# Attention scores as 64-row products of two heads, one run per key chunk, behind a hold

## The chip, the cores and the metric

The kernel runs on one core of one Trainium2 chip. The metric is the device time of one execution in microseconds (us); the time before is the median of three runs, 2896.34 us (2895.69 to 2900.71).

A core has TensorE (PE; its weight loads are listed as PEld), VectorE (DVE), ScalarE (ACT), GpSimd (POOL) and a queue engine (SP) that issues the transfers. PE writes its results to PSUM, eight banks of 512 float32 columns on 128 partitions, and each engine takes its instructions in a fixed order.

## What is computed

Two layers over 2048 tokens with 16 learned meta tokens in front, model width 1024, all in float32. Layer 0 runs sliding-window attention and a convolution branch side by side. Layer 1, which the change is about, is stick-breaking attention with 16 heads of 64:

```python
z = jnp.einsum('bqhd,bkhd->bhqk', qp[:, i * BLOCK:kend], kp[:, :kend]).astype(jnp.float32) * scale
log_beta = jax.nn.log_sigmoid(z)
log_1m = jnp.where(valid, jax.nn.log_sigmoid(-z), 0.0)
after = lax.cumsum(log_1m, axis=3, reverse=True) - log_1m
a = jnp.where(valid, jnp.exp(log_beta + after), 0.0)
outs.append(jnp.einsum('bhqk,bkhd->bqhd', a.astype(v.dtype), vp[:, :kend]))
```

Each query's weight on a key is sigmoid(z) of that key times the product of sigmoid(-z) over all later keys. The output is gated by SiLU, projected, normalized and added to the input.

## The kernel before

Matrix products whose precision matters are split: an operand is a high part in the short float32r format plus a low part, and `mm3` adds high x high, low x high and high x low. A projection unit is one output block of 128 features for up to 512 tokens: 8 x 3 = 24 products into one PSUM tile `pj`, then read by ACT (`ev`), and for most kinds by DVE.

Layer 1 works by head pair `p` (0 to 7; two heads `h`, 64 rows each) and half of the tokens `hf`. Inside, `pair_steps(m)` takes 256 queries (two blocks `x` of 128) and walks their keys backwards in chunks of at most four blocks of 128 (`edges`), which gives 8 chunks for a head pair in the first half of the tokens and 16 in the second, 192 in all. One chunk has four score tiles, `(h, x)`. For each:

- PE: `z` (L912), two products of 128 rows. The stationary side is a query tile that holds the high (then the low) part of one head's queries twice, in rows 0 to 63 and 64 to 127; the moving side `kst` holds that head's keys, high part above low part. So one product gives high x high plus high x low.
- ACT: two sigmoids of it, `om` (L919) and `be` (L920). POOL masks the diagonal block in a pair's first chunk (L923).
- DVE: a scan along the keys, `S` (L925), then `be` times `S` (L926).
- PE: transposes of `be` into `pt` (L944); ACT copies them to `aT` (L950).

When all four are through, PE multiplies the transposed weights with the values into `av` (L958). Those products use half of the array's columns each, one head in either half (`128*64` in the profile). A row's `128*128` or `128*64` gives the rows and columns of the array that a product takes.

The order on each engine is made by a scheduler at build time, from the order of the calls, from priorities (`high_priority`) and from its own estimate of times. `interleave` calls projection units of a later head pair between the chunks of the current one; `behind` ties a unit to the value products of a few chunks before. A PSUM tile waits for the last reader of the tile that had its bank. The banks before are `pj` 2, `pz` 3 (scores), `pt` 2 (transposes), `pav` 1.

Of the kernel before, what the change touches and what calls it, by code (L numbers as in the profile page):

```python
# [18 lines left out]
P = 128  # L19
# [16 lines left out]
PB = (2, 3, 2)  # L36
# [42 lines left out]
class Trunk:  # L79
# [113 lines left out]
    def layer0(self, after=None):  # L193
# [300 lines left out]
        def cbranch(ut):  # L494
# [44 lines left out]
            def pw():  # L539
# [91 lines left out]
        def outp(t):  # L631
# [3 lines left out]
            def mm(nh):  # L635
# [9 lines left out]
                ps = self.bank("pj", "po")  # L645
# [92 lines left out]
    def after0(self, pool, tags):  # L738
        self.layer1_pools()
        self.evs = (pool, tags, D, 2)  # L740
        self.H, self.gates, self.tags = {}, [], cycle(("raw", "wh", "wl", "wh", "wl"))
# [9 lines left out]
        def proj(p, hf, parts=(0, 1)):  # L751
# [11 lines left out]
            def unit(m, part, c0, n, evac):  # L763
                def go():
# [4 lines left out]
                    ps = self.bank("pj", "pj1")  # L769
# [54 lines left out]
    def layer1(self):  # L824
# [12 lines left out]
        def attn(p, hf):  # L837
# [43 lines left out]
            def qload(m):  # L881
                q0 = NM + m * 2 * P
                S["q"] = qs = []
                for h in range(2):
                    for i in range(2):
                        qt = w2.tile([P, 256], F32R, tag=f"q{h}{i}", name="qt")
                        for j in range(2):
                            self.mv(qt[j * HD : j * HD + HD], qd[i][p, h * HD : h * HD + HD, q0 : q0 + 256])
                        qs.append(qt)

            def pair_steps(m):
# [5 lines left out]
                def chunk(ei):  # L897
# [6 lines left out]
                    nbs = [b1 - b0 - (1 if first else 0), b1 - b0]  # L904
                    for h in range(2):
                        for x in range(2):
# [3 lines left out]
                            z = self.bank("pz", "z")  # L910
                            for i in range(2):
                                nc.tensor.matmul(z[:, :n], S["q"][2 * h + i][:, x * P : x * P + P], S["k"][h][:, k0 : k0 + n], start=(i == 0), stop=(i == 1))  # L912
# [7 lines left out]
                            nc.scalar.activation(be[:, :n], z[:, :n], AF.Sigmoid, scale=0.125)  # L920
# [10 lines left out]
                    cps, avs = [], []  # L931
                    for c in range(0, b1 - b0, 2):
                        cw = min(2, b1 - b0 - c)
                        aTs = []
                        for h in range(2):
# [9 lines left out]
                            aT = w4.tile([P, 512], F32, tag="aT", name="aT")  # L945
# [5 lines left out]
                            aTs.append(aT)  # L951
# [182 lines left out]
```

## Time and profile before

| | |
|---|---|
| Median of three runs | 2896.34 us (2895.69 to 2900.71) |
| Profiled execution, its own time | 2902.22 us |
| Its span, first to last instruction | 2900.5 us |
| Granted TensorE clock in it, mean | 0.982 |
| Busy: PE, PEld, DVE, ACT, POOL | 2735.1, 2193.5, 2209.4, 1472.3, 777.6 us |
| Score products (L912) | 1536, 394.9 us busy |
| Transposes (L944) | 2176, 363.2 us busy |
| Value products (L958) | 2304, 282.0 us busy |
| Scans (L925) | 536.6 and 204.8 us busy in two groups |

A group's row reads: line, engine, operation, tile written and tiles read, shapes, count, busy time, mean of one in ns, then the idle time before them on that engine with what ended it. A timeline row reads: start, duration, engine, line, operation, tiles, count; neighbours of one kind are merged. PE's durations overlap, because a product starts before the one ahead of it has left the array, so its busy time overstates how full it is: what a product costs is the distance between starts.

### The profile page before, as it was taken

The page shows a single profiled execution, that of the slowest core. Times are in us where ns is not written, and L with a number is a line of the kernel's source. Part 1 is how long each engine was busy: PE and PEld are TensorE (multiplying, and loading weights), DVE is VectorE, ACT ScalarE, POOL GpSimd, SP SyncE. Part 2 cuts the span into 40 slices and gives each one's busy share as a digit, 9 for nine tenths or more (in the row PEclk, how much of TensorE's full clock was granted, in tenths as well). Part 3 has the DMA queues.
Part 4 walks back from the last instruction along what each step waited for, and adds up shares of the span by engine and source line. Part 5 has one row for each costly group of instructions (what it writes and reads, how often), then busy time and mean ns, then how long its engine had stood idle before and what let it go on. Part 6 is the DMA issues. An engine that isn't in the chain of part 4 may idle for free.

```text
span 2900.5 us, 49605 instructions
## 1 busy us (share of the span) xinstructions
PE 2735.1 (94%) x16110; PEld 2193.5 (76%) x16110; DVE 2209.4 (76%) x3696; ACT 1472.3 (51%) x3574; POOL 777.6 (27%) x2679
## 2 busy tenths in 40 slices
PE   7888999999899999999999899999999999999997
PEld 7886777777688799888887677777777777766876
DVE  7987888888767744666668987878888887887864
ACT  4223434343545323455445656666666766665551
POOL 3431212000000212333335532323223322333210
PEclk9999999999999999999999999999999999999999
DMA  7877888788876664444446462423232342244322
GB/s 258 283 251 221 254 267 256 234 241 267 235 209 187 213 199 146 130 127 137 128 137 182 130 178 65 113 76 101 66 103 88 88 111 73 74 129 126 113 95 91
DMA packets 303986, 462.87 MB, mean 160 GB/s; under 512 B 46640, under 2 KB 200640, under 8 KB 300656
## 3 DMA queue, kind: packets, MB, share of 16 engines
q1 hardware_dynamic: 303728, 459.70, 52.5%
q8 instruction: 129, 2.11, 0.3%
q14 instruction: 129, 1.06, 0.1%
HBM read 312.16 MB, written 142.14 MB: 157 GB/s over the span
## 4 chain that ended last, share of the span: by engine, by line
PE 71%; DVE 10%; DMA 7%; issue 4%; ACT 4%; POOL 2%; SPq 1%; DVEq 0%; ACTq 0%; POOLq 0%
PE pj L142 11%; PE pj L144 11%; PE pj L143 11%; PE z L912 8%; PE av L958 7%; PE pt L944 7%; PE po L142 4%; PE po L144 4%; PE po L143 4%; DVE y L309 3%; DVE S L925 2%; DMA qs<-qr 1%; DVE be L926 1%; DMA raw<-in_w_in 1%; ACT om L919 1%
## 5 line engine op out<-in xcount | busy, mean ns | idle before, releaser
L925 DVE TENSOR_TENSOR_SCAN S<-om,be 128x401 f32<-128x401 f32 (+3 forms) x512 | 536.6, 1069 | 71.9 <-ACT om L919 51.3
L919 ACT ACTIVATE om<-z 128x384 f32<-128x384 f32 (+5 forms) x768 | 377.9, 510 | 196.7 <-PE z L912 131.8
L926 DVE TENSOR_TENSOR be<-be,S 128x385 f32<-128x385 f32 (+5 forms) x768 | 413.6, 563 | 76.0 <-POOL be L917 22.2
L142 PE MATMUL pj<-th,wh 128*128 128x512 f32 (+2 forms) x1280 | 460.5, 360 | 7.1 <-DVE ev L810 3.6
L144 PE MATMUL pj<-th,wl 128*128 128x512 f32 (+2 forms) x1280 | 452.8, 354 | 0.0
L143 PE MATMUL pj<-tl,wh 128*128 128x512 f32 (+2 forms) x1280 | 450.5, 352 | 0.0
L950 ACT COPY aT<-pt 128x512 f32<-128x512 f32 (+2 forms) x672 | 334.2, 504 | 196.6 <-PE pt L944 156.2
L912 PE MATMUL z<-kst,qt 128*128 128x384 f32 (+6 forms) x1536 | 394.9, 357 | 31.2 <-ACT be L920 29.8
L920 ACT ACTIVATE be<-z 128x384 f32<-128x384 f32 (+5 forms) x768 | 375.5, 505 | 72.7 <-PE pt L944 72.0
L309 DVE SCALAR_TENSOR_TENSOR y<-u,cw,y 128x512 f32<-128x512 f32 (+1 forms) x480 | 391.7, 828 | 6.1
L944 PE MATMUL pt<-ident,be 128*128 128x128 f32 x2176 | 363.2, 282 | 17.4 <-ACT ev L799 7.7
L944 PEld LDWEIGHTS pt<-ident,be 128*128 128x128 f32 x2176 | 253.6, 142 | 113.0 <-issue 31.0
L912 PEld LDWEIGHTS z<-kst,qt 128*128 128x128 f32 x1536 | 247.7, 190 | 75.7 <-ACT be L920 55.3
L958 PE MATMUL av<-aT,vt 128*64 128x256 f32 (+1 forms) x2304 | 282.0, 380 | 4.3 <-DVE og L976 4.3
L916 POOL MEMSET om<- 128x1 f32 x768 | 74.8, 99 | 768.6 <-DVE S L925 753.5
L144 PE MATMUL pj<-hTh,wl 128*128 128x512 f32 (+2 forms) x704 | 246.7, 353 | 23.9 <-POOL wl L132 16.9
L142 PEld LDWEIGHTS pj<-th,wh 128*128 128x128 f32 x1280 | 241.8, 189 | 33.9 <-DVE ev L810 4.6
L144 PEld LDWEIGHTS pj<-th,wl 128*128 128x128 f32 x1280 | 241.0, 188 | 29.9
L143 PEld LDWEIGHTS pj<-tl,wh 128*128 128x128 f32 x1280 | 241.4, 189 | 25.1 <-issue 0.4
L142 PE MATMUL pj<-hTh,wh 128*128 128x512 f32 (+2 forms) x704 | 249.6, 356 | 8.9 <-DMA wh<-wk 4.6
L925 DVE TENSOR_TENSOR_SCAN S<-om 128x257 f32<-128x257 f32 (+4 forms) x256 | 204.8, 812 | 63.1 <-POOL om L923 50.3
L143 PE MATMUL pj<-hTl,wh 128*128 128x512 f32 (+2 forms) x704 | 246.8, 351 | 0.8 <-DVE hTl L191 0.8
(184 smaller groups left out, 4702.2 us busy)
## 6 DMA issues: line engine op xcount, KB each, us to landing
raw<-in_w_in SPq DMA_DIRECT2D x98, 512.0 KB, 4.0
wr<-wk SPq DMA_DIRECT2D x44, 512.0 KB, 6.2
wh<-wk SPq DMA_DIRECT2D x44, 512.0 KB, 5.2
wl<-wk SPq DMA_DIRECT2D x44, 512.0 KB, 6.5
qt<-qhd SPq DMA_DIRECT2D x256, 64.0 KB, 2.6
qt<-qld SPq DMA_DIRECT2D x256, 64.0 KB, 2.4
wk<-wh SPq DMA_DIRECT2D x22, 512.0 KB, 4.9
wk<-wl SPq DMA_DIRECT2D x22, 512.0 KB, 4.9
```

What stands on the lines that cost most here:

```text
L142: mm(out, sh, mh, start=first, stop=False)
L143: mm(out, sh, ml, start=False, stop=False)
L144: mm(out, sl, mh, start=False, stop=last)
L309: return lambda: nc.vector.scalar_tensor_tensor(y[:, :TC], u[:, w : w + TC], cw[:, j, w : w + 1], y[:, :TC], ALU.mult, ALU.add)
L912: nc.tensor.matmul(z[:, :n], S["q"][2 * h + i][:, x * P : x * P + P], S["k"][h][:, k0 : k0 + n], start=(i == 0), stop=(i == 1))
L919: nc.scalar.activation(om[:, :n], z[:, :n], AF.Sigmoid, scale=-0.125)
L920: nc.scalar.activation(be[:, :n], z[:, :n], AF.Sigmoid, scale=0.125)
L925: nc.vector.tensor_tensor_scan(P_[:, : n + 1][:, ::-1], om[:, : n + 1][:, ::-1], om[:, : n + 1][:, ::-1], init, ALU.mult, ALU.bypass)
L926: nc.vector.tensor_tensor(bl[:, : n + 1], bl[:, : n + 1], P_[:, : n + 1], ALU.mult)
L944: nc.tensor.transpose(pt[:, o : o + P], bes[h, x][:, mo + b * P : mo + b * P + P], self.ident)
L950: cps.append(nc.scalar.copy(aT[:, lo:hi], pt[:, lo:hi]))
L958: mi = nc.tensor.matmul(av[h * HD : h * HD + HD, qc0 + x0 : qc0 + 256], S["v"][:, b0 + b, h * HD : h * HD + HD], at, start=not S["started" ...
```

## The change

The score products are cut to 64 rows. The query tiles are now one for the high and one for the low part with both heads, head 0 in rows 0 to 63 and head 1 below, and so are the key tiles. For each block `x`, three products per head (high x high, high x low, low x high) are called in turn for the two heads, each head in its half of the array's rows and with a PSUM bank of its own. All products of a chunk are called ahead of its sigmoids, in one run of twelve. The first of them gets a wait for the last four readings of score banks (`zread`) and for the copies of the transposes of the chunk ahead's first head (`half`). The transposes are called head by head. PSUM is split anew: `pj` 1, `pz` 4. Projections in layer 0, and the output projections outside of attention, alternate between `pj` and `pz`; those among attention use the one `pj` bank.

```diff
-PB = (2, 3, 2)
+PB = (1, 4, 2)
...
-                    ps = self.bank("pj", "pw")
+                    ps = self.bank(next(banks), "pw")
...
-                ps = self.bank("pj", "po")
+                ps = self.bank(next(banks), "po")
...
+        self.zread, self.half, self.free = [], [], cycle(BK)
...
-                    ps = self.bank("pj", "pj1")
+                    ps = self.bank(next(self.free), "pj1")
...
-                for h in range(2):
+                for i in range(2):
                     kst = w4.tile([P, T], F32R, tag="kst", name="kst")
-                    for i in range(2):
-                        self.mv(kst[i * HD : i * HD + HD, :n], kd[i][p, h * HD : h * HD + HD, :n])
+                    self.mv(kst[:, :n], kd[i][p, :, :n])
...
-                for h in range(2):
-                    for i in range(2):
-                        qt = w2.tile([P, 256], F32R, tag=f"q{h}{i}", name="qt")
-                        for j in range(2):
-                            self.mv(qt[j * HD : j * HD + HD], qd[i][p, h * HD : h * HD + HD, q0 : q0 + 256])
-                        qs.append(qt)
+                for i in range(2):
+                    qt = w2.tile([P, 256], F32R, tag=f"q{i}", name="qt")
+                    self.mv(qt, qd[i][p, :, q0 : q0 + 256])
+                    qs.append(qt)
...
+                    zs, wait = {}, self.zread[-4:] + self.half
+                    for x in range(2):
+                        n = nbs[x] * P + mo
+                        if n == 0:
+                            continue
+                        for h in range(2):
+                            zs[h, x] = self.bank("pz", "z")
+                        for i, j in ((0, 0), (0, 1), (1, 0)):
+                            for h in range(2):
+                                r = slice(h * HD, h * HD + HD)
+                                mi = nc.tensor.matmul(zs[h, x][:, :n], S["q"][i][r, x * P : x * P + P], S["k"][j][r, k0 : k0 + n], start=(i + j == 0), stop=(i == 1))
+                                if wait is not None:
+                                    self.after_all(mi, wait)
+                                    wait = None
...
-                            z = self.bank("pz", "z")
-                            for i in range(2):
-                                nc.tensor.matmul(z[:, :n], S["q"][2 * h + i][:, x * P : x * P + P], S["k"][h][:, k0 : k0 + n], start=(i == 0), stop=(i == 1))
+                            z = zs[h, x]
...
-                            nc.scalar.activation(be[:, :n], z[:, :n], AF.Sigmoid, scale=0.125)
+                            self.zread.append(nc.scalar.activation(be[:, :n], z[:, :n], AF.Sigmoid, scale=0.125))
...
-                    for c in range(0, b1 - b0, 2):
-                        cw = min(2, b1 - b0 - c)
-                        aTs = []
-                        for h in range(2):
+                    cps, aTs = [], {}
+                    for h in range(2):
+                        for c in range(0, b1 - b0, 2):
+                            cw = min(2, b1 - b0 - c)
...
+                        if h == 0:
+                            self.half = cps[:]
...
-                ps = self.bank("pj", "po1")
+                ps = self.bank(next(self.free), "po1")
...
+        self.free = cycle(("pj",))
         for p in range(2, 6):
             interleave(proj(p, 0), attn(p - 2, 0))
...
+        self.free = cycle(BK)
         for t in range(8, NT):
```

How this moves the work shows in the order on PE. In the rows, `z` are score products (with the lengths of their key rows), `pt` transposes, `av` value products, `pj` projections; a count at the end merges equal neighbours. First a place in the second half of the tokens where no projection unit is called. Before:

```order
L912 MATMUL z<-kst,qt 128x400 x2
L944 MATMUL pt_24352<-ident,be 128x128 x4
L912 MATMUL z<-kst,qt 128x256 x2
L912 MATMUL z<-kst,qt 128x384 x2
L958 MATMUL av_24083<-aT,vt_23339 64x256 x8
L944 MATMUL pt_24359<-ident,be 128x128 x4
L912 MATMUL z<-kst,qt 128x256 x2
L944 MATMUL pt_24366<-ident,be 128x128 x4
```

Now:

```order
L913 MATMUL z<-kst,qt 128x400 x12
L953 MATMUL pt_20045<-ident,be 128x128 x3
L953 MATMUL pt_20052<-ident,be 128x128 x3
L953 MATMUL pt_20160<-ident,be 128x128 x4
L969 MATMUL av_19877<-aT,vt_19865 64x256 x8
L953 MATMUL pt_20167<-ident,be 128x128 x2
L953 MATMUL pt_20172<-ident,be 128x128 x4
L953 MATMUL pt_20179<-ident,be 128x128 x2
L913 MATMUL z<-kst,qt 128x256 x6
```

Before, the next chunk's scores (256 and 384 columns) stand between the transposes of the chunk ahead, tile by tile. Now the chunk's own transposes (`pt_20160` and after) all stand ahead of the next chunk's scores.

Second, a place where a projection unit ends. Before:

```order
L944 MATMUL pt_24729<-ident,be 128x128 x2
L142 MATMUL pj_24938<-th_18069,wh_24820 128x512
L143 MATMUL pj_24938<-tl_18070,wh_24820 128x512
L144 MATMUL pj_24938<-th_18069,wl_24821 128x512
L142 MATMUL pj_24938<-th_18069,wh_24820 128x512
L143 MATMUL pj_24938<-tl_18070,wh_24820 128x512
L144 MATMUL pj_24938<-th_18069,wl_24821 128x512
L912 MATMUL z<-kst,qt 128x512 x2
L944 MATMUL pt_24788<-ident,be 128x128 x4
L912 MATMUL z<-kst,qt 128x400 x4
L958 MATMUL av_24083<-aT,vt_23339 64x256 x6
```

Now:

```order
L953 MATMUL pt_20293<-ident,be 128x128 x3
L953 MATMUL pt_20300<-ident,be 128x128
L143 MATMUL pj_20491<-tl_17399,wh_20487 128x512
L144 MATMUL pj_20491<-th_17398,wl_20488 128x512
L953 MATMUL pt_20304<-ident,be 128x128 x4
L953 MATMUL pt_20311<-ident,be 128x128
L913 MATMUL z<-kst,qt 128x384 x12
L969 MATMUL av_19877<-aT,vt_19865 64x256 x4
```

Before, the last scores of one chunk and then scores of the next follow the unit, around transposes of the chunk ahead. Now the unit, the transposes of both heads, the twelve scores of the next chunk and the value products stand in line.

More of the change, by code (lines that the diff above doesn't have):

```diff
@@ L944, in chunk @@
                                         nc.tensor.transpose(pt[:, o : o + P], bes[h, x][:, mo + b * P : mo + b * P + P], self.ident)
-                            aT = w4.tile([P, 512], F32, tag="aT", name="aT")
+                            aTs[h, c] = aT = w4.tile([P, 512], F32, tag="aT", name="aT")
                             if nbs[0] < c + cw and cw == 2:
@@ L950, in chunk @@
                                 cps.append(nc.scalar.copy(aT[:, lo:hi], pt[:, lo:hi]))
-                            aTs.append(aT)
-                        for b in range(c, c + cw):
-                            o = (b - c) * 256
-                            x0 = 0 if b < nbs[0] else P
-                            avs += [(h, b, x0, aTs[h][:, o + x0 : o + 256]) for h in range(2)]
+                        if h == 0:
+                            self.half = cps[:]
+                    avs = []
+                    for b in range(b1 - b0):
+                        c, x0 = b - b % 2, 0 if b < nbs[0] else P
+                        o = (b - c) * 256
+                        avs += [(h, b, x0, aTs[h, c][:, o + x0 : o + 256]) for h in range(2)]
                     with tc.high_priority(offset=AVP):
```

1 line of the change is left out of this document (removed).

## The prediction

> **What bounds the kernel now.** I read the page's busy shares and chain first, then busy time by stage, the groups of the attention stage, and the timeline of one pass.
>
> ```profile
> PE 2735.1 (94%) x16110; PEld 2193.5 (76%) x16110; DVE 2209.4 (76%) x3696; ACT 1472.3 (51%) x3574; POOL 777.6 (27%) x2679
> PE 71%; DVE 10%; DMA 7%; issue 4%; ACT 4%; POOL 2%; SPq 1%; DVEq 0%; ACTq 0%; POOLq 0%
> 1269.00:1346.00 77.00, 75.93 (x534) 65.63 (x535) 48.21 (x80) 39.05 (x116) 29.52 (x117) 1.00 0.46 132
> 1961.00:2091.00 130.00, 125.59 (x757) 93.30 (x757) 107.83 (x141) 87.53 (x210) 38.50 (x182) 1.00 0.32 90
> 2618.00:2809.00 191.00, 187.16 (x1021) 147.29 (x1023) 150.50 (x233) 102.21 (x228) 51.10 (x188) 0.98 0.35 108
> ```
>
> The last three rows give length, then PE, PEld, DVE, ACT, POOL busy. The first is one head pair's attention over the first half of the tokens (8 key chunks); call it a short pass. The second is a long pass (second half, 16 chunks), the third the last long pass, filled with output projections. PE leads everywhere; in the long pass DVE is close behind. But PE's busy time counts overlapping ends. What it can issue is read from starts:
>
> ```profile
> 2003.21 0.40 PE L144 MATMUL pj<-th,wl 128*128 128x512 f32 x1
> 2003.45 0.39 PE L142 MATMUL pj<-th,wh 128*128 128x512 f32 x1
> 2003.68 0.39 PE L143 MATMUL pj<-tl,wh 128*128 128x512 f32 x1
> 2003.91 0.39 PE L144 MATMUL pj<-th,wl 128*128 128x512 f32 x1
> ...
> 1990.01 1.95 PE L958 MATMUL av<-aT,vt 128*64 128x256 f32 x16
> 1991.88 0.66 PE L944 MATMUL pt<-ident,be 128*128 128x128 f32 x4
> ...
> 2018.89 0.60 PE L944 MATMUL pt<-ident,be 128*128 128x128 f32 x4
> 2019.25 1.17 PE L912 MATMUL z<-kst,qt 128*128 128x512 f32 x4
> 2020.35 1.52 PE L958 MATMUL av<-aT,vt 128*64 128x256 f32 x12
> 2021.80 0.66 PE L944 MATMUL pt<-ident,be 128*128 128x128 f32 x4
> 2022.21 0.72 PE L912 MATMUL z<-kst,qt 128*128 128x512 f32 x2
> ```
>
> A 512-column product starts 0.233 us after the last, 0.45 ns a column; a projection unit of 24 is 5.6 us. Four transposes of 128 columns take 0.41 (2021.80 to 2022.21), 0.10 each. A value run of 16 takes 1.87 us to the next start, one of 12 takes 1.45: 0.21 for each two of 256 columns, what one alone would take at a transpose's rate, so the two heads, each in half of the array's columns, run at the same time. 0.19 is fixed. Transposes and scores before it, 2018.89 to 2020.35, take 1.46, where 4 x 0.10 and 4 x 0.233 make 1.33: 0.13 to enter. So a round trip into another tile shape costs about 0.3 us, 0.15 a switch.
>
> By these prices and the order's counts a long pass holds 119 us of PE work (eight projection units 45, scores 23, transposes 21, values 21, switches 5, small ones 4), a short one 74.6. The short pass is PE's; the long one has 11 us of slack, which shows as these waits (us in total) in it:
>
> ```profile
> PEld z L912 <- ACT be L920: 5.7, 12, 1.1
> DVE S L925 <- ACT om L919: 3.7, 4, 1.7
> PE z L912 <- ACT be L920: 2.8, 6, 0.9
> ```
>
> They are small because score products run up to a chunk and a half ahead of the transposes, one bank at a time, so DVE nearly always has a filled bank.
>
> **Part 1, fewer score slots.** By `edges`, a long pass has 51,712 product columns (23.3 us), a short one 18,944 (8.5 us). Four full-height products become three side-by-side pairs, so a quarter goes, if a pair takes one slot: 5.8 us a long pass, 2.1 a short one, 63 us over eight of each. The value pairs above are the nearest row, and I take one slot. The other bound is two slots, with no overlap at all: scores would then cost half as much again as before instead of a quarter less.
>
> The Trainium skill's page "TensorE: Matmul & The Clock Gate", section "LDWEIGHTS (loading the stationary operand)", says that a load's time goes by its columns, 128 at about 107 ns, whatever its rows. By that, a pair whose two loads came one after the other would take 0.21 us, the estimate for a 384-column pair going from 0.17 to 0.21, and most of the 63 us would be gone, the sum below some 50 us higher. This trace agrees for full height, two loads about 0.11 us apart (0.30 for two, each 0.19):
>
> ```profile
> 2004.83 0.30 PEld L912 LDWEIGHTS z<-kst,qt 128*128 128x128 f32 x2
> ```
>
> No row here shows half-height loads, so that stays inside the bounds.
>
> **Part 2, tile switches.** The order of PE has 488 changes of tile shape before and 853 after: 365 x 0.15 = 55 us of PE time (47 to 69 by 0.13 and 0.19). Parts 1 and 2 leave PE about 8 us ahead over the program: 1.4 in a long pass, nothing in a short one.
>
> **Part 3, the hold.** This is the term that decides. A score run now waits for all eight sigmoids of the chunk before it and for the copies of that chunk's first head. PE takes its products in order, so the value products, projections and transposes behind the run wait too, and ACT, POOL and DVE wait for its scores. In the built order 143 of 191 score runs stand even behind the chunk's last transposes; the other 48 are split around the second head's. After such a run of the first kind DVE has been dry since its last multiplication. The rows for the restart:
>
> ```profile
> 2004.86 0.61 PE L912 MATMUL z<-kst,qt 128*128 128x400 f32 x2
> 2005.51 0.50 ACT L919 ACTIVATE om<-z 128x400 f32<-128x400 f32 x1 [0.17 <-PE z L912]
> ...
> 2007.81 0.51 ACT L919 ACTIVATE om<-z 128x400 f32<-128x400 f32 x1
> 2008.41 1.05 DVE L925 TENSOR_TENSOR_SCAN S<-om,be 128x401 f32<-128x401 f32 x1 [0.85 <-POOL be L917]
> ...
> L919 ACT ACTIVATE om<-z 128x384 f32<-128x384 f32 x256 | 132.4, 533 | 73.7 <-PE z L912 55.3 <-DVE S L925 12.9 <-PE ptv L798 2.5
> L923 POOL TENSOR_SCALAR_AFFINE_SELECT om<-om 128x128 f32<-128x128 f32 x256 | 131.9, 519 | 63.7 <-ACT om L919 62.1
> ```
>
> From the run's start: three pairs 0.54, 0.3 for the last result and a hop (two scores from 2004.86 are issued by 2005.22, the sigmoid starts 2005.51), one sigmoid 0.53, a hop of 0.1 (sigmoid's end 2008.32, scan 2008.41): 1.45 us, plus 0.5 of POOL's select in a pair's first chunk. Before the run come a hop, five or six transposes and a switch: 0.8. So the gap is 2.2 us for a run of the first kind, and about 0.25 for a split one; the ends are no gap at all (the first rival) and 2.2 at all sixteen chunks, 35 us a long pass. DVE's own work for a chunk:
>
> ```profile
> L925 DVE TENSOR_TENSOR_SCAN S<-om,be 128x401 f32<-128x401 f32 x160 | 166.2, 1058 | 32.1 <-ACT om L919 25.1 <-POOL be L917 6.8
> L925 DVE TENSOR_TENSOR_SCAN S<-om,be 128x513 f32<-128x513 f32 x128 | 163.3, 1292 | 13.4 <-ACT om L919 12.4
> L925 DVE TENSOR_TENSOR_SCAN S<-om,be 128x385 f32<-128x385 f32 x160 | 159.3, 1015 | 22.6 <-issue 11.6 <-ACT om L919 10.7
> L926 DVE TENSOR_TENSOR be<-be,S 128x385 f32<-128x385 f32 x256 | 142.1, 570 | 14.0 <-POOL be L923 5.1 <-POOL be L917 1.6 <-issue 0.9
> L926 DVE TENSOR_TENSOR be<-be,S 128x513 f32<-128x513 f32 x128 | 90.5, 739 | 15.2 <-POOL be L917 10.1 <-ACT be L920 2.2
> L926 DVE TENSOR_TENSOR be<-be,S 128x401 f32<-128x401 f32 x160 | 88.8, 578 | 16.1 <-POOL be L917 9.6 <-POOL am L929 1.8 <-ACT be L920 1.0
> ```
>
> Four scans and four multiplications: 8.1 us for 512 keys, 6.5 for 400, 6.3 for 384. The long pass in the new order has eight chunks with a projection unit between their scores and their last transposes: 5.6 + value products 1.3 + transposes 1.2 + scores 0.9 + switches 0.5 + 0.3 for the small ones = 9.8 us of PE, more than DVE's 8.2 to 8.6 there, so 78 us. The other eight have no projection: three of 512, three of 400, two of 384 keys, 56.4 us of DVE; five restarts of 1.45 (7.3), two closing waits of 0.8 and some split gaps of 0.25 add 10: 66 us, in which PE has 4 us of work a chunk and idles. Together 144 against 130 now: the two engines no longer run past each other. DVE's remaining 10 us a pass (107.8 less these groups) fall into gaps or PE-bound chunks; I cost them at nothing, and up to 5 a pass if that cover fails.
>
> Six such passes give 84. The seventh (2481 to 2618, already 137 us) gives 8, and the last, PE's, nothing. In the short passes PE work per chunk, 6 to 16 us, exceeds DVE's path almost everywhere; two chunks fall short, 1.5 us a pass. Two short passes with few projections (1584 to 1703) give 3.
>
> **Part 4, one projection bank.** A unit's first product now waits until the one before it is read. That needs, for 512 columns, these two plus hops, 1.7 us:
>
> ```profile
> L782 ACT CAST ev<-pj 128x512 fp32r<-128x512 f32 x48 | 28.2, 588 | 71.2 <-PE pj L144 65.9 <-issue 3.6 <-DMA qt<-qhd 1.6
> L783 DVE TENSOR_TENSOR ev<-pj,ev 128x512 fp32r<-128x512 f32 x48 | 33.1, 689 | 48.9 <-ACT ev L782 48.9
> ```
>
> In long passes the order has 2.9 us or more of other PE work at each of the eight boundaries: nothing. In short ones, twelve boundaries have 0.5 to 3.0, short by 3.5 us in all at worst; I take 0.5 of it, since the same pass already counts its idle chunks. Short passes: 2 x 6 = 12. Layer 0's projections alternate between one bank and four instead of two and three: its score banks gain what the projection banks lose; I take 3, between -10 and +15.
>
> **Part 5, loads.** Queries go from eight transfers to two per block pair, keys from four to two:
>
> ```profile
> qt<-qhd SPq DMA_DIRECT2D x256, 64.0 KB, 2.6
> ```
>
> They are prefetched and no wait above names one: nothing. SP's queue only gets shorter.
>
> **Sum.** 84 + 8 + 12 + 3 + 3 = 110 on the profiled execution's 2902.2 us: 3012. The median of the three runs is 5.9 lower, so 3006 us, 3.8% slower.
>
> **Rivals.** *The hold is cheap (faster).* If the copies come so early that the next scan follows the last multiplication within some 0.3 us, the four-bank runs take away the waits on z's banks instead: 5.7 + 2.8 = 8.5 us at most in a long pass, 60 over seven, plus PE's 8. Half of that gives 2896 - 34 = 2862; I put it at 2870. It decides where the split runs are the rule; against it stand 143 of 191 that are not. *Gain and loss cancel.* PE's 8 us against stalls of that size: 2896. For it: 0.15 a switch is an estimate. *Pairs do not overlap.* Scores double against my sum: 8.5 x 0.75 = 6.4 us in each short pass, about 11 in a long one (restarts lengthen too): 120 more, 3126. Against it: value pairs overlap in 12- and 16-runs. This is also the case in which the change does not do what it says.
>
> **Chances.** Serialized by the hold 0.70, its own range 2935 to 3075 (the idle terms halved, or with DVE's 5 a pass and 1.5 of Part 4); hold cheap 0.17; cancel 0.06; no overlap 0.07. A measurement of this kernel can tell about 0.2%: slower 0.77, same 0.06, faster 0.17. The range 2868 to 3075 leaves out the 0.07, half of the cheap-hold case and the ends of the first.
>
> **What would show it.** Right: long passes near 144 us with PE's share lower, DVE's idle time before the scans grown and put down to ACT's `om`, and ACT's to PE's z; short passes near 79. Score pairs starting nanoseconds apart would settle Part 1; the start gaps at both ends of a score run Part 2. If long passes stay at or under 130 us, Part 3 is wrong; if z's matmuls start one slot apart within a pair, Part 1.

## The result, and the profile after

The changed kernel takes 3260.22 us (median of four runs, 3256.83 to 3263.39), the kernel before on the same chip 2898.53 us: a ratio of 1.124, 95% interval 1.121 to 1.127. The forecast was slower, at 3006. So the sign was right, and the loss is 362 us where 110 were forecast.

The page's busy shares and row of granted clocks after:

```profile
PE 2880.7 (88%) x16878; PEld 2219.6 (68%) x16878; DVE 2191.2 (67%) x3696; ACT 1455.0 (45%) x3568; POOL 760.1 (23%) x2679
PEclk9999999999999999999888888989888889889999
```

Every engine's share is lower: nothing became the bound. And the granted clock falls below 0.9 in most slices of the second half, which the page before shows nowhere. The three stretches that answer to those of before (short pass, third long pass, last long pass; length, then busy time of PE, PEld, DVE, ACT, POOL, then granted clock, DMA share, GB/s):

```profile
1260.00:1342.60 82.60, 78.53 (x563) 63.88 (x563) 47.33 (x80) 38.54 (x116) 28.43 (x117) 1.00 0.34 110
2104.00:2276.00 172.00, 139.09 (x810) 96.97 (x806) 105.60 (x140) 86.67 (x209) 36.77 (x181) 0.87 0.18 60
2987.00:3172.00 185.00, 175.14 (x993) 128.91 (x992) 139.24 (x216) 95.31 (x220) 41.20 (x169) 0.96 0.26 82
```

Short pass 77 to 82.6, long pass 130 to 172, last long pass 191 to 185. The whole program in five stages, cut at first scans: all up to the end of the first short pass, the seven other short passes, six long passes, the seventh, the last with the tail. First before, then after:

```profile
0.00:1192.00 1192.00, 1100.52 (x6158) 920.27 (x6158) 900.07 (x1842) 470.65 (x1062) 219.22 (x394) 0.97 0.74 229
1192.00:1703.00 511.00, 493.82 (x3325) 413.63 (x3324) 354.57 (x554) 269.31 (x784) 224.29 (x829) 0.99 0.50 144
1703.00:2481.00 778.00, 750.92 (x4511) 557.19 (x4509) 646.55 (x841) 523.09 (x1257) 227.54 (x1079) 1.00 0.33 93
2481.00:2618.00 137.00, 126.14 (x740) 93.93 (x738) 118.88 (x148) 87.39 (x209) 49.19 (x189) 0.97 0.37 110
2618.00:2900.50 282.50, 263.72 (x1381) 208.45 (x1381) 189.36 (x314) 121.82 (x265) 57.41 (x193) 0.97 0.32 102
```

```profile
0.00:1177.00 1177.00, 1099.51 (x6245) 917.48 (x6246) 897.12 (x1844) 467.04 (x1065) 223.24 (x405) 0.98 0.74 231
1177.00:1764.00 587.00, 527.53 (x3545) 413.38 (x3546) 347.23 (x553) 263.29 (x780) 213.72 (x825) 0.95 0.35 113
1764.00:2796.00 1032.00, 848.09 (x4899) 591.41 (x4896) 640.10 (x840) 523.66 (x1262) 223.61 (x1083) 0.87 0.19 63
2796.00:2987.00 191.00, 149.86 (x826) 103.12 (x825) 123.91 (x153) 87.29 (x213) 50.78 (x193) 0.86 0.29 94
2987.00:3261.70 274.70, 255.72 (x1369) 194.24 (x1367) 182.86 (x308) 113.78 (x255) 48.76 (x177) 0.97 0.28 89
```

The differences: -15, +76, +254, +54, -8, together +361. In the six long passes DVE does the same 640 us in 1032 instead of 778. PE's busy time there grows by 97 us, although a quarter of the score slots is gone, at a clock of 0.87 instead of 1.00. The groups after of the scans (DVE) and transposes (PE) say what was waited for; the part behind the second bar is the engine's idle time ahead of the group and what ended it:

```profile
L935 DVE TENSOR_TENSOR_SCAN S<-om,be 128x401 f32<-128x401 f32 (+3 forms) x512 | 536.0, 1071 | 220.2 <-ACT om L929 219.2 <-POOL am L939 0.3 <-ACT be L930 0.2
L935 DVE TENSOR_TENSOR_SCAN S<-om 128x257 f32<-128x257 f32 (+4 forms) x256 | 203.4, 814 | 177.6 <-POOL om L933 176.9 <-POOL be L927 0.4 <-POOL om L926 0.2
L953 PE MATMUL pt<-ident,be 128*128 128x128 f32 x2176 | 408.9, 310 | 243.4 <-DVE be L936 171.6 <-ACT aT L959 69.9 <-ACT ev L800 0.6
```

The scans wait for scores (398 us of idle in both groups; in the second by way of POOL, which masks the sigmoid's result), the transposes for what DVE makes of the scans (172): PE and DVE take turns. One turn, in the third long pass, on PE (start, duration, what ran, count, idle before and its releaser):

```profile
2112.48 1.65 PE L913 MATMUL z<-kst,qt 64*128 64x512 f32 x12
2114.06 1.30 PE L969 MATMUL av<-aT,vt 128*64 128x256 f32 x12
2116.62 0.41 PE L953 MATMUL pt<-ident,be 128*128 128x128 f32 x2 [1.26 <-DVE be L936]
2119.49 1.12 PE L953 MATMUL pt<-ident,be 128*128 128x128 f32 x6 [2.46 <-DVE be L936]
2121.36 0.66 PE L953 MATMUL pt<-ident,be 128*128 128x128 f32 x2 [0.75 <-ACT aT L959]
2121.95 2.37 PE L913 MATMUL z<-kst,qt 64*128 64x400 f32 x12
...
2129.01 3.68 PE L969 MATMUL av<-aT,vt 128*64 128x256 f32 x16
2132.62 1.65 PE L953 MATMUL pt<-ident,be 128*128 128x128 f32 x8
```

The first row also settles Part 1: twelve products of 512 columns take 1.58 us to the next start, six slots of 0.233 and 0.18 for the shape, so a pair takes one slot. Then PE idles 1.26, 2.46 and 0.75 us, and what follows is slow: twelve products of 400 columns take 2.30 us, more than those of 512 did, and sixteen value products 3.61, which took 1.87 before.

### The profile page after: what moved, and what is told of

Same layout as the page of the kernel before. It is cut to its first block, busy times and chain, and to the rows that moved or that the text cites. A ratio compares the mean times of both kernels' runs of the same rounds, so it can differ in the third digit from the quotient of the medians.

```text
span 3261.7 us, 50235 instructions
## 1 busy us (share of the span) xinstructions
PE 2880.7 (88%) x16878; PEld 2219.6 (68%) x16878; DVE 2191.2 (67%) x3696; ACT 1455.0 (45%) x3568; POOL 760.1 (23%) x2679
## 5 line engine op out<-in xcount | busy, mean ns | idle before, releaser
L953 PE MATMUL pt<-ident,be 128*128 128x128 f32 x2176 | 408.9, 310 | 243.4 <-DVE be L936 171.6
L959 ACT COPY aT<-pt 128x512 f32<-128x512 f32 (+2 forms) x672 | 305.3, 502 | 611.7 <-PE pt L953 570.4
L953 PEld LDWEIGHTS pt<-ident,be 128*128 128x128 f32 x2176 | 277.5, 154 | 391.7 <-DVE be L936 130.8
L142 PE MATMUL pj<-th,wh 128*128 128x512 f32 (+2 forms) x1280 | 471.7, 369 | 13.2 <-DVE ev L811 7.1
L936 DVE TENSOR_TENSOR be<-be,S 128x385 f32<-128x385 f32 (+5 forms) x768 | 398.4, 541 | 21.1 <-POOL am L939 0.3
L930 ACT ACTIVATE be<-z 128x384 f32<-128x384 f32 (+5 forms) x768 | 391.0, 509 | 0.0
L969 PE MATMUL av<-aT,vt 128*64 128x256 f32 (+1 forms) x2304 | 320.0, 419 | 1.5 <-ACT aT L959 1.5
L913 PE MATMUL z<-kst,qt 64*128 64x384 f32 (+6 forms) x2304 | 298.3, 393 | 4.4 <-ACT aT L957 3.8
L143 PEld LDWEIGHTS pj<-tl,wh 128*128 128x128 f32 x1280 | 245.0, 191 | 29.7 <-issue 2.3
L913 PEld LDWEIGHTS z<-kst,qt 64*128 64x128 f32 x2304 | 211.2, 215 | 55.6 <-issue 39.4
L969 PEld LDWEIGHTS av<-aT,vt 128*64 128x64 f32 x2304 | 164.8, 152 | 121.3 <-issue 50.0
```

The source lines that it names most:

```text
L142: mm(out, sh, mh, start=first, stop=False)
L143: mm(out, sh, ml, start=False, stop=False)
L913: mi = nc.tensor.matmul(zs[h, x][:, :n], S["q"][i][r, x * P : x * P + P], S["k"][j][r, k0 : k0 + n], start=(i + j == 0), stop=(i == 1))
L930: self.zread.append(nc.scalar.activation(be[:, :n], z[:, :n], AF.Sigmoid, scale=0.125))
L936: nc.vector.tensor_tensor(bl[:, : n + 1], bl[:, : n + 1], P_[:, : n + 1], ALU.mult)
L953: nc.tensor.transpose(pt[:, o : o + P], bes[h, x][:, mo + b * P : mo + b * P + P], self.ident)
```

## The experiments

Each kernel ran beside the kernel before on the same chip (medians of before 2897.8 to 2905.4 us). Several chips were used, so a difference of a few us between two kernels is better read from the ratios. "Long pass" is the third, cut at first scans.

| kernel | median us | ratio to before, 95% | long pass us, clock |
|---|---|---|---|
| before | 2898.53 | | 130, 1.00 |
| changed | 3260.22 | 1.121 to 1.127 | 172, 0.87 |
| no hold | 3030.17 | 1.043 to 1.047 | 146, 1.00 |
| hold on sigmoids alone | 3023.07 | 1.041 to 1.046 | 150, 0.94 |
| hold, full-height products | 3212.61 | 1.106 to 1.110 | 164, 0.91 |
| before + PSUM split | 2924.76 | 1.006 to 1.011 | 135, 0.99 |
| gaps filled, coarse | 3320.01 | 1.142 to 1.147 | 176, 0.92 |
| full height, no hold | 2898.88 | 0.998 to 1.000 | 130, 1.00 |
| runs of six, no more hold | 2956.57 | 1.017 to 1.022 | 137, 1.00 |
| before + alternating banks | 2903.13 | 1.000 to 1.002 | 130, 1.00 |
| gaps filled, fine | 3199.90 | 1.101 to 1.107 | 162, 0.97 |
| changed, units of 256 | 3160.46 | 1.088 to 1.094 | 155, 0.96 |
| full height, no hold, units of 256 | 2865.75 | 0.987 to 0.992 | 124, 1.00 |
| full height, no hold, banks shared | 2878.27 | 0.990 to 0.995 | 130, 1.00 |
| both of these | 2832.98 | 0.974 to 0.977 | 124, 1.00 |
| hold on sigmoids, units of 256 | 2912.27 | 1.001 to 1.005 | 130, 0.99 |
| runs of six, units of 256 | 2919.21 | 1.004 to 1.006 | 132, 1.00 |

**No hold.**

```diff
-                    zs, wait = {}, self.zread[-4:] + self.half
+                    zs, wait = {}, None
```

> The changed kernel with the hold taken away and nothing else: the 64-row pairs, the PSUM split and the head-by-head transposes stay. In the built order 173 of 191 score runs now stand ahead of the previous chunk's transposes (before the change 147, after it none), and PE changes tile shape 1446 times (488 before, 853 after). Theory A (the hold puts PE, ACT and DVE into one chain, and in the gaps the granted clock falls as well): the gaps go, long passes return to 125 to 140 us at a clock of 1.00; 958 switches more than before at 0.15 us are 144 us of PE, less 63 us of saved score slots, less what slack takes up: 2900 to 2990 in all. Rival B (the 64-row products and their tile switches cost the time, not the hold): 593 switches more than in the changed kernel make it slower still, 3300 or more. Rival C (one projection bank and four score banks cost it): about 3260, as with the hold.

3030: 230 us of the loss go with the hold, and the clock in the long passes is back at 1.00. It misses A's range above by 40, and the order shows why: nothing keeps a run together any more. Its PE timeline in a long pass:

```profile
2045.08 0.79 PE L913 MATMUL z<-kst,qt 64*128 64x384 f32 x3
2045.80 0.44 PE L953 MATMUL pt<-ident,be 128*128 128x128 f32 x2
2046.17 0.80 PE L913 MATMUL z<-kst,qt 64*128 64x384 f32 x3
```

The three products of one head now stand alone between transposes: 0.72 us for three slots of 0.175 and the switches, with half of the array's rows empty. So the hold has a use: it keeps the pairs paired.

**Hold on the sigmoids alone.**

```diff
-                    zs, wait = {}, self.zread[-4:] + self.half
+                    zs, wait = {}, self.zread[-4:]
```

> The changed kernel with half of the hold: a score run waits for the sigmoids of the chunk before it, but no longer for the copies of that chunk's first head. In the built order 167 of 191 runs stand whole ahead of the previous chunk's transposes; 1070 tile switches. Theory A (what costs is that the run stands behind the transposes, so that DVE has nothing to scan while PE transposes, and PE nothing to do while DVE scans): long passes 125 to 140 us, clock back at 1.00, 2850 to 2940 in all. A weaker form of A (any wait for the whole earlier chunk serializes): 3100 or more. Rival B (rows and switches): 217 switches more than in the changed kernel, about 3290. Rival C (PSUM split): about 3260.

3023: 237 us go with the wait for the first head's copies. That is A by sign, 80 us above its range, below the weaker form: a wait for the whole chunk's eight sigmoids still costs something where projections come in lumps (long pass 150 at 0.94).

**Full-height products, hold kept.** The products as before, two a tile, in one run of eight behind the hold.

```diff
-                        for i, j in ((0, 0), (0, 1), (1, 0)):
-                            for h in range(2):
...
+                        for h in range(2):
+                            for i in range(2):
+                                mi = nc.tensor.matmul(zs[h, x][:, :n], S["q"][2 * h + i][:, x * P : x * P + P], S["k"][h][:, k0 : k0 + n], start=(i == 0), stop=(i == 1))
```

> The changed kernel with the score products of full height again (two products for each head and query block, hi and lo stacked in 128 rows, four in a run where the pairs made six), and everything else kept: one run per chunk, the hold, the PSUM split, head-by-head transposes. 497 tile switches, 153 of 191 runs behind the previous chunk's last transposes. Theory A: 3200 to 3290, long passes 165 to 178 us at a clock under 0.92: nearly all of the loss is the hold's. Rival B (rows and switches): 2900 to 2990. Rival C (PSUM split): 3200 to 3290 too; the run of the split alone tells it from A.

3213, in A's range (long pass 164 at 0.91). **The same without the hold** has both edits shown. **The PSUM split in the kernel before** takes the split and the bank lines of the change, with projections in the attention on the one bank:

```diff
-PB = (2, 3, 2)
+PB = (1, 4, 2)
...
-                    ps = self.bank("pj", "pj1")
+                    ps = self.bank(next(self.free), "pj1")
```

> The changed kernel without the hold and with full-height score products: what is left of the change is the PSUM split, the code order of one run per chunk and the head-by-head transposes. 497 tile switches. Beside the run with the 64-row products and no hold (3030) it tells what unpaired 64-row products cost: that order has only 424 side-by-side pairs and 1456 products alone between transposes, and its scores take 42 us of PE in a long pass against 24 where pairs stay whole. Theory A: 2900 to 2945, as the PSUM split alone (2925), long passes 132 to 137. Rival (the head-by-head transposes cost by themselves, through the two transpose banks): 2960 to 3030.

> The kernel before with the PSUM split of the change alone: one projection bank instead of two and four score banks instead of three, with the projections of the first layer and of the tail alternating over both sets of banks, as the change has it. Score products, their order and the transposes as before. Theory A and rival B: the split is worth little in the attention, the fourth bank takes away some of the 8.5 us of score waits of a long pass, the single bank costs up to 12 us in the short ones, and layer 0 shows most of the 24.7 us that the changed kernel has there: 2880 to 2930. Rival C: the split carries most of the loss, 3100 or more.

2899, just under A's range, and 2925, inside its own. These settle the sum: split, code order and head-by-head transposes together cost nothing (0.998 to 1.000), the hold on top of them 314 us, the 64-row pairs on top of that 48. The six long passes of the kernel without and with the hold:

```profile
1691.00:2473.00 782.00, 746.46 (x4500) 557.59 (x4501) 644.10 (x840) 525.07 (x1257) 213.88 (x1078) 1.00 0.32 92
1763.00:2744.00 981.00, 827.24 (x4528) 619.03 (x4526) 639.84 (x842) 517.79 (x1262) 220.79 (x1082) 0.90 0.25 73
```

Same instructions, same DVE work; 199 us more, of which PE reports 81 as busy, at 0.90.

**Runs of six.** Each block's six products wait for the two sigmoids that free their banks; the rest goes block by block.

```diff
+                        wait = self.zread[-4:-2] if x == 0 else self.zread[-2:]
                         for h in range(2):
                             zs[h, x] = self.bank("pz", "z")
```

> The changed kernel with the hold cut to what keeps pairs whole: each query block's six products wait for the two sigmoids that free their two banks, sigmoids, scans and so on go block by block, no wait for a transposed head. 1111 pairs, 82 products alone, 1144 tile switches; nearly all runs stand ahead of the previous chunk's transposes. Theory A: DVE is fed half a chunk earlier than with the wait for all eight sigmoids (3023), so gaps mostly go; a long pass then is PE's: 129 at before's work, 5.8 less for the pairs, 291 more switches than the changed kernel spread over all, some 12 more in all against before: 135 to 142 us, 2920 to 2980. Rival (a run of pairs that waits for two banks at once dries DVE as much as the whole hold of sigmoids): 3020 or more.

2957: in A's range. Against full height (2899) the pairs themselves cost 58 us where nothing is held beyond their banks.

**Alternating banks in the kernel before**: the bank lines alone, `PB` still (2, 3, 2).

> The kernel before with one thing of the change: layer 0's second half, layer 1's first projections and the last output projections alternate between the projection and the score banks; the split stays 2, 3, 2. In the runs with one, four and two banks the first short pass ended 15 to 33 us earlier than before, although its first scan came 25 us later. If the alternation does that, this kernel is faster than before: 2860 to 2890, the first short pass ending by 1165. If the split does it, or the alternation only moves the wait: 2890 to 2925.

2903: no effect. The earlier end of the first short pass is not the alternation's alone.

**Filling the gaps, coarse, then fine.** Both add products whose results nothing reads. The fine one puts them, by a table made from the gaps of the changed kernel's trace, ahead of a chunk's first transpose and behind it:

```diff
+                    def dummy(n):
+                        for _ in range(n):
+                            nc.tensor.matmul(zs[0, 0][:, :256], S["q"][0][:, :P], S["k"][0][:, :256], start=True, stop=True)
+                    dummy(fill[0])
...
+                                        if (h, c, b, x) == (0, 0, 0, 0):
+                                            with tc.issue_after(getattr(tr, "ins", tr)):
+                                                dummy(fill[1])
```

> The changed kernel with more work for PE: in the long passes each chunk without a projection unit gets 24 further products of 256 columns, whose results nothing reads, between its score run and its transposes (1959 in all, by the 0.45 ns a column some 28 us of PE in each long pass, where the changed kernel's trace has 32 us of gaps over 0.3 us and 172 us at a granted clock of 0.87). Theory A1 (the gaps cost twice: PE idles, and the granted clock then falls, so that the products of the serial chain after a gap take up to twice their time): the clock in the long passes rises to 0.96 or more, a pass falls to 148 to 162 us although PE does more, and the time is 3060 to 3190. Rival A2 (the chain's waits alone make the loss, and the low clock falls on work that would have waited anyway): what does not fit the gaps comes on top, 3262 to 3400.

> The changed kernel with its gaps filled where its trace has them: in 60 chunks of the long passes extra products of 256 columns, whose results nothing reads, fill 0.7 of the gap before the chunk's first transpose and of the gap between its first transposes; 817 in all, 94 us of PE by 0.45 ns a column, 12 us a long pass against 28 in the first filling, half of which stood in chunks with a projection unit. Here 593 of the 817 stand in chunks without one. Theory A1 (the gaps cost twice, since the granted clock falls in them): long passes at a clock of 0.93 or more and 150 to 166 us against 172, 3090 to 3220 in all, although PE does more. Rival A2 (the low clock falls on work that would have waited anyway): long passes 171 us or more, 3255 to 3350.

The coarse filling gave 3320, in A2's range, and its third long pass took 176 us at a clock of 0.92, where A1 had 148 to 162. It decides little: nearly half of its products stood in chunks that were PE's already, and 44 of its 60 us more fall in the last long pass and the tail (319 us against 275), which output projections fill. The fine one gave 3200: with 94 us more work for PE the kernel is 60 us faster, as A1 has it, and A2 falls. The same chunk, one with a projection unit, in the changed kernel and in the filled one, and the chunk after the gaps shown above in both:

```profile
2173.05:2188.77 15.72, 14.21 (x72) 10.29 (x72) 5.79 (x9) 5.28 (x15) 3.89 (x15) 0.73 0.05 18
2121.95:2134.20 12.25, 10.34 (x49) 6.66 (x48) 5.92 (x8) 5.41 (x13) 3.14 (x14) 0.52 0.13 44
```

```profile
2159.16:2169.72 10.56, 10.56 (x68) 8.18 (x68) 5.79 (x9) 4.82 (x14) 3.97 (x14) 1.00 0.07 26
2113.14:2123.00 9.86, 9.18 (x58) 6.89 (x58) 6.23 (x9) 5.62 (x13) 3.15 (x14) 0.79 0.69 253
```

The first has no extra product in it and takes 10.6 us instead of 15.7, at a clock of 1.00 instead of 0.73: the chunk ahead, with extra products in its gaps, left the clock up. So the low clock lies on the path.

**Units of 256 columns.** The second half's projections in shorter units, one in nearly each chunk, with the change whole and, as a control, at full height without the hold:

```diff
-[[(1040, 512)], [(1552, 512)]]]
+[[(1040, 256), (1296, 256)], [(1552, 256), (1808, 256)]]]
```

> The changed kernel, hold and pairs kept, with layer 1's second-half projections cut into units of 256 columns instead of 512, so that the order has one of 24 shorter products (2.8 us) in nearly each chunk of a long pass, where it had a unit of 5.6 us in every second one. The PE work is about the same. Theory A (the hold makes PE's and DVE's work of a chunk follow one another; a long pass is the sum over chunks of the larger of PE's work and DVE's with its restart, and the gaps slow PE's clock as well): with PE work of some 7 us in each chunk the eight chunks of 12.1 us become shorter, the eight without a projection lose their gaps of 3.3 us and the low clock: long passes 138 to 155 us, clock 0.95 or more, 2970 to 3110 in all. Rival (the serial chain costs the same wherever the projections stand): long passes 165 us or more, 3200 to 3280.

> Control for the run with units of 256 columns: the same cut in the kernel with full-height products and no hold (2899). There PE and DVE run past each other anyway, so where the projections stand should matter little: 2885 to 2930, more evacuations and weight loads against nothing gained. If it fell below 2880, the cut would be worth something by itself, and the gain under the hold would have to be read against that.

3160 and 2866. Spreading takes 100 us off the changed kernel and 33 off the control, which was forecast to gain nothing; why the control's long passes fall to 124 was not separated. Under the hold the time missed its range by 50, although the long pass (155 at 0.96) is at the end of its own: more than lumps of projections is left. **The same with the hold on the sigmoids alone**, and **with runs of six**, tell what:

> Units of 256 columns and 64-row pairs, with the hold on the eight sigmoids alone: no wait for the transposed head. With the whole hold this was 3160, long passes 156 us; without hold and pairs 2866, 124 us. If the wait for the transposed head is most of what is left even with the projections spread: 2930 to 2990, long passes 132 to 140. Rival (a wait for the whole chunk's scores is enough to serialize): 3060 or more.

> Units of 256 columns with 64-row pairs in runs of six and no more wait than their two banks need (with units of 512: 2957, long passes 137). Against the same with full-height products (2866, 124 us) it prices the 64-row pairs themselves where PE is the bound: 652 tile switches more, 54 in a long pass, at 0.15 us 8 us, less 5.8 us of saved slots: 127 to 131 us and 2890 to 2920 in all. If the pairs cost what they cost with units of 512 (58 us): 2915 to 2935. If 2866 or less, the pairs would pay where nothing is held.

2912 and 2919. The wait for the transposed head is 248 of the 295 us between 3160 and 2866, more than forecast. The wait for eight sigmoids costs nothing once the projections are spread (2912 with it, 2919 in runs of six), and the pairs cost 53 (2919 against 2866; 46 by the ratios, since the two ran on different chips). 2919 lies in both ranges given for the runs of six, so it does not choose between them. The changed kernel with spread units and the kernel with the hold cut to the sigmoids, third long pass:

```profile
2093.00:2248.00 155.00, 133.45 (x1009) 105.33 (x1008) 106.90 (x146) 87.41 (x218) 37.84 (x179) 0.96 0.21 69
1958.00:2088.00 130.00, 126.64 (x1012) 101.36 (x1011) 107.64 (x147) 89.81 (x218) 38.30 (x181) 0.99 0.25 83
```

**A version that beats both.** Full height, no hold, split 1, 4, 2; in the short passes projections use both sets of banks, first alone, then with units of 256:

```diff
-        self.free = cycle(("pj",))
         for p in range(2, 6):
...
+        self.free = cycle(("pj",))
         for p in range(NPR - 3):
```

> A version that may beat both: full-height products, no hold, PSUM split 1, 4, 2, head-by-head transposes (2899 with projections held to the one bank in the attention), but projections alternating between the projection bank and the score banks through the short passes as well; only the long passes keep the one bank. In that run the second to eighth short pass took 531 us against 511 before, long passes 130 as before, the start some 32 us less. If the one bank is what costs in the short passes: 531 falls to about 511 and the time to 2875 to 2890. If not: 2895 to 2910.

> A version that may beat both kernels by more: full-height products without a hold, PSUM split 1, 4, 2, with both of what gained alone: projections of the second half in units of 256 columns (2866 with it, 2899 without) and projections alternating over both sets of banks in the short passes (2878 with it). The first acts on the long passes (124 us against 130), the second on the short ones (506 against 531), so they should add: 2840 to 2850.

2878 and 2833: the gains add, by somewhat more than forecast, and the last is 2.5% faster than the kernel before. It keeps of the change the PSUM split, the order of calls and the head-by-head transposes, and neither the pairs nor the hold.

## Why the prediction was right in sign and wrong in size

**Part 1** was right: a pair takes one slot (1.58 us for six of 512 columns), a quarter of the slots goes. Nor does a pair pay for two loads one after the other. A run at full clock in the changed kernel:

```profile
2143.88 1.32 PE L913 MATMUL z<-kst,qt 64*128 64x384 f32 x12
2145.13 1.30 PE L969 MATMUL av<-aT,vt 128*64 128x256 f32 x12
```

Its six pairs take 1.25 us, six times 0.175 and 0.2; at 0.21 a pair they would have taken 1.46.

**Part 2** had the price about right and the balance wrong by little. At units of 256 the pairs cost 46 to 53 us; with the 63 saved, 652 more switches cost 109 to 116, 0.17 to 0.18 us each if all lie on the path and the block-by-block order costs nothing, inside 0.13 to 0.19. By that the changed kernel's 356 more than at full height (497 to 853) cost about 60 and the pairs come out even. Measured under the hold they cost 48 (3213 to 3260), with the long passes at a clock of 0.87 instead of 0.91. That fits PE's saved work turning into gaps, but no run separates it.

**Part 3 is the step that failed, in size.** Its mechanism stands: the hold makes the engines take turns, DVE waits for `om`, transposes for DVE. It was mis-sized in all its terms: six long passes 84 forecast, +254 measured, of which 199 are the hold's own at full height (782 us without it, 981 with it); the seventh 8, and +54, of which 28 (147 and 175); the seven short passes 15 with Part 4, and +76, of which 54 (531 and 585). Only the last pass, nothing forecast, was right (-8 with the tail). What the working left out is the clock. It took every price of PE from a trace at 1.00, gave PE 4 us of work in each of the eight chunks of some 8.2 us without a projection, and did not ask what the clock does then. The third long pass after, its eight chunks with a projection unit and the eight without, summed from score run to score run:

```profile
sum 96.88, PE 90.46 PEld 66.24 DVE 49.77 ACT 43.53 POOL 24.40; mean PE 11.31 PEld 8.28 DVE 6.22 ACT 5.44 POOL 3.05
sum 75.38, PE 48.89 PEld 30.79 DVE 56.73 ACT 43.67 POOL 12.59; mean PE 6.11 PEld 3.85 DVE 7.09 ACT 5.46 POOL 1.57
```

Forecast were 78 and 66. The five projection chunks at a clock of 1.00 take 9.68 to 11.05 us, 10.4 in the mean against the 9.8 priced; the three at 0.73 to 0.78 take 13.4 to 15.8. Of the chunks without one, those at 0.94 and above take 7.2 to 9.8, the two at 0.52 and 0.72 take 12.2 and 11.9. At 10.4 the eight would take 83: 14 of the 19 us too many there are the clock's.

The eight without a projection are DVE's. In the chunk of the timeline above it works without a break from 2114.40 to 2121.8, so PE's three waits there (1.26, 2.46, 0.75) do not lengthen that chunk; they lower the clock for the next. What counts is how long DVE stands dry from a chunk's last multiplication to the next chunk's first scan. Behind that chunk, and behind the one after it:

```profile
2124.01 1.05 DVE L935 TENSOR_TENSOR_SCAN S<-om,be 128x401 f32<-128x401 f32 x1 [2.19 <-ACT om L929]
2135.63 0.78 DVE L935 TENSOR_TENSOR_SCAN S<-om 128x257 f32<-128x257 f32 x1 [5.60 <-POOL om L933]
```

Six of these eight waits are 1.3 to 2.2 us, about the 2.2 priced for a run of the first kind; none is as short as the 0.25 of a split run. The other two, behind the chunks at 0.52 and 0.72, are 5.6 and 5.3: value products and transposes, slowed by the clock, still stand between DVE's last multiplication and the next scores. In the filled kernel those two chunks take 9.9 and 8.3 us instead of 12.2 and 11.9. The clock is not shown to be the whole: with the fine filling at 0.97 a long pass is still 162, against 144 forecast and 130 without a hold. It holds some 12 us of extra products, and how much of the rest is theirs and how much the turn's was not separated.

The seventh pass and the short ones were costed by "PE's work exceeds DVE's path". In the seventh, transposes waited 25.0 us for DVE (no such wait before) and scans 48.6 for scores (2.7 before); in the seven short passes transposes waited 29.7 us for DVE (1.0 before). So the turns are there too.

**Part 4** was right in kind: one projection bank costs 20 to 26 us in the seven short passes (531 and 505 with and without it, 511 before), where Part 4 had 0.5 in each of six, 3 of the 12 forecast. Layer 0's +3 hides two larger terms: the first scan comes 25 us later, the first short pass takes 40 less, -15 in all. **Part 5** was right: no wait in the long pass names a load.

Of the rivals, "the hold is cheap" and "gain and loss cancel" fall with the hold's 314 us, "pairs do not overlap" with the timeline, though it comes true where a scheduler breaks the runs (no hold: 131 us more than at full height).

## What to carry to other kernels

A wait that ties a producer's next run to the consumer's result turns two overlapped engines into a chain; price the chain in turns, and then price PE's work in it at the clock that those gaps leave, not at the clock of the busy profile. If pairs must stay together, hold them on what frees their banks and on nothing later. And fill the turn evenly: projection units half as long were worth 33 us without any hold and 100 with it.

## What the runs showed of the hardware

Extra work made the kernel faster: 817 unread products, 94 us of PE time, took 60 us off, by lifting the clock of the six long passes from 0.87 to 0.95. And the clock fell after short gaps. The waits of transposes for DVE in the third long pass of the changed kernel (total, count, longest):

```profile
PE pt L953 <- DVE be L936: 19.5, 16, 2.5
```

No gap of PE in that pass is longer than 2.5 us, yet the chunk after the gaps shown above ran at 0.52. The Trainium skill, page "TensorE: Matmul & The Clock Gate", section "Why this matters for your kernels", asks for no idle gaps over about 3 us, or the clock halves. The halving agrees (sixteen value products 3.61 us, 1.87 before); the length does not, if single gaps are counted. The same page's section "Part 4: PE-mode transpose" says that transposes do not count as PE work for the clock in the same way. By that the stretch from 2115.36 to 2121.95, with ten transposes and nothing else, counts as 6.6 us idle, and the rule would hold. The kernel before tells the two readings apart. At the start of its last long pass PE waited 2.65 us and then ran sixteen transposes and nothing else:

```profile
2618.03 3.56 PE L944 MATMUL pt<-ident,be 128*128 128x128 f32 x16 [2.65 <-ACT ev L799]
2614.40:2617.82 3.42, 0.97 (x7) 0.54 (x5) 3.42 (x5) 0.74 (x4) 3.37 (x5) 1.00 0.64 215
2617.82:2621.23 3.41, 3.20 (x15) 2.85 (x16) 3.32 (x5) 1.97 (x6) 3.06 (x10) 0.50 0.70 213
2621.23:2624.64 3.41, 3.41 (x27) 2.46 (x27) 1.71 (x4) 3.41 (x9) 2.45 (x9) 1.00 0.85 298
```

The clock fell at the end of a gap of 2.65 us and was back at 1.00 after 3.4 us with transposes alone. If they did not count, PE would have stood idle until 2621.34 and the clock should have stayed down. So here they count, and a limit of about 3 us on single gaps does not fit: the clock fell at gaps of 2.65 and 2.5. The stretch ahead of the fall in the changed kernel looks alike:

```profile
2116.56:2119.97 3.41, 0.89 (x6) 0.69 (x7) 3.41 (x4) 0.94 (x2) 0.26 (x4) 1.00 1.02 401
2119.97:2123.39 3.42, 2.67 (x14) 1.95 (x14) 1.85 (x3) 1.16 (x2) 0.13 (x2) 0.50 0.80 333
```

In both, PE was busy for less than a third of the 3.4 us before the clock fell (0.97 and 0.89 us). How much work would have kept it up was not measured.
